# Three of seven inner products of an MLP's second product, taken for both token halves at once by a second seven-product scheme

## The chip, the cores and the metric

The kernel runs on one core of one Trainium2 chip. The metric is the device time of one execution in microseconds. A core has TensorE (PE: matmuls, with weight loads shown as PEld), VectorE (DVE), ScalarE (ACT), GpSimd (POOL) and SyncE (SP), which here issues nearly all DMAs. Each engine works off its own queue of instructions in order; they wait for each other at semaphores.

## The reference

One layer of an encoder over 2048 tokens of width 1024: a mixer (two kinds of attention, output projection, residual), then an MLP. Only the MLP matters here:

```python
h = rmsnorm(x, g_norm2[l]) * (1.0 + sc2) + sh2
x = x + gt2 * (jnp.square(jax.nn.relu(h @ w1[l])) @ w2[l])
```

w1 is 1024 x 4096, w2 is 4096 x 1024, all in float32.

## The kernel before

Everything is held transposed: features on the 128 partitions, tokens along the free axis, in four token blocks of 512 (`TB`). The MLP takes the tokens in two halves, `mb` 1 and then 0, each of two blocks. Within a half, each of the two MLP products is split into 2 x 2 blocks (output rows by tokens by contraction), and a Strassen-Winograd scheme makes the four block results from seven block products instead of eight. They are numbered 1 to 7 and taken in the order `PRODUCTS = (1, 6, 5, 7, 2, 3, 4)` (line 1283). The operands of products 3, 5, 6, 7 are sums and differences of blocks.

Precision: a float32 operand is split into two float32r parts, hi and lo (`split`, line 139: a cast on ScalarE, then a subtraction on VectorE), and `mm3` (line 206) issues three matmuls: hi by hi, hi by lo, lo by hi. Each is a 128 x 128 stationary tile against 512 moving columns.

The MLP is a list `steps` of objects, run in order by the loop at the end (line 1738 on). Before a step is run, its successors are prepared, that is, their operands split, as long as no more than eight operand tiles (pool `opp`, line 1289) are in use; each class says how many it takes and frees (`tiles`, `frees`). Jobs hung to a step number with `at(n, job)` (line 1325) are issued just before that step's matmuls; `later` holds jobs for some steps after. TensorE and SP keep the order of the program. The two classes of the MLP:

- `First` (line 1425), product with w1. A step is one product of one of 16 pairs of hidden tiles: 4 contraction tiles x 3 matmuls. The moving operands of all seven products stay in SBUF (`hops`, made by `right_blocks`, line 1363). The stationary sums are made on GpSimd (`sums`, line 1457). Relu, square and the sums that the second product needs of the hidden tiles are made on ScalarE and VectorE, and stored to DRAM as `scr_hid[mb, product, pair]` (`keep`).
- `Second` (line 1545), product with w2. A step is one of 16 contraction tiles of one product: 4 row blocks x 3 matmuls into four PSUM banks. Operands come from DRAM, two steps at a time: hidden tiles from `scr_hid`, weights from w2 or from the weight sums `scr_s` (`load`, line 1554), into one of four 8 KB buffers (`raw_pair`, line 1305). After a product's last step, `out` (line 1605) takes the banks: products 1, 6, 5, 7 build the running sums that Winograd's scheme needs (`s`, `u`, `v`, in the 12 buffers of `kept`), and 7, 2, 3, 4 finish an output block: `scalar_tensor_tensor` multiplies by the gate and adds to x, which `load_base` and `base` have brought in and to which they have added the running sum.

The weight sums `scr_s` are made once, during `First` of half 1, by `second_sums` (line 1525): per pair, four sums on VectorE and their stores. `norm2` (line 1331) computes the RMS norm of one token block: 8 loads, squares on ScalarE, adds on VectorE, four small matmuls (tile `pvm`), an inverse root on GpSimd, a diagonal on VectorE, four matmuls that spread it (tile `psr`). For half 0 it is hung at `end - 8` and `end`, `end` being the border between `First` and `Second` of half 1 (lines 1685, 1686), and `right_blocks` for half 0 follows at `end + 16 + 10 k`. The norm's and x's tiles come from `temp`, seven buffers.

In the profile's names: `oph`, `opv` are the split hidden and weight operands of `Second`, `opw` those of `First`, `w2s` the tile of `second_sums`, `tx` the x tiles, `ty` and `h` the right blocks, `ts` and `w` the sums of w1 on GpSimd. All instructions carry line 42, a helper's, so that groups are told apart by tile names.

Of the kernel before, what the change touches and what calls it, by code (L numbers as in the profile page):

```python
# [79 lines left out]
def encoder_kernel(ctx, tc, xT, c, g1, g2, w_in, w_rest, gqk, bias, w_o, w1, w2, w_ada, b_ada, out):  # L80
# [1200 lines left out]
    NP = DFF // P // 2  # L1281
    HK = KT // 2
    PRODUCTS = (1, 6, 5, 7, 2, 3, 4)
    scr_hid = scratch("scr_hid", [P, 2, TB], 2, 8, NP // 2)
    scr_s = scratch("scr_s", [P, 2, TB], 7, NP // 2)

    pm = ctx.enter_context(ExitStack())
    if True:
# [36 lines left out]
        def at(n, job):  # L1325
            jobs.setdefault(n, []).append(job)
# [4 lines left out]
        def norm2(tb, step):  # L1331
# [213 lines left out]
        class Second(Step):  # L1545
# [27 lines left out]
            def run(self):  # L1573
                mb, i, j = self.mb, self.i, self.j
                if j == 0:
                    Second.banks[i] = [bank(f"{self.nm}_{n}") for n in range(HK)]
                if i not in (1, 6, 5):
                    if j == NP // 2 - 1:
                        self.load_base()
                    if NP // 2 + 2 < j <= NP // 2 + 2 + HK:  # L1580
                        self.base(j - NP // 2 - 3)
# [10 lines left out]
            def load_base(self):  # L1592
                i, d = self.i, Second.whole
                for n in range(HK):
                    d["x", n] = temp(f"x{self.nm}_{n}")
                    sp.dma_start(d["x", n], scr_x[2 * self.mb + (i in (2, 4)), n + HK * (i in (7, 4))])

            def base(self, n):

                i, d = self.i, Second.whole  # L1600
                nn = n + HK * (i in (7, 4))
                x, u = d["x", n], d[{7: "v", 2: "s", 3: "v", 4: "u"}[i], n]
                dve.scalar_tensor_tensor(x, u, mod[:, 5 * KT + nn : 5 * KT + nn + 1], x, op0=ALU.mult, op1=ALU.add)

            def out(self, n, ps):
                i, d = self.i, Second.whole
                tb = 2 * self.mb + (i in (2, 4))
# [4 lines left out]
                if i == 6:  # L1612
                    d["u", n] = column_sum(dve, kept(f"u{self.nm}_{n}"), ps, d["s", n], ALU.add)
                    return
                if i == 5:
                    d["v", n] = column_sum(dve, kept(f"v{self.nm}_{n}"), ps, d["u", n], ALU.add)
                    return
                if i == 7:
                    column_sum(dve, d["u", n], ps, d["u", n], ALU.add)
                nn = n + HK * (i in (7, 4))  # L1620
                x = d["x", n]
                dve.scalar_tensor_tensor(x, ps, mod[:, 5 * KT + nn : 5 * KT + nn + 1], x, op0=ALU.mult, op1=ALU.add)
                sp.dma_start(out[nn * P : (nn + 1) * P, tb * TB : (tb + 1) * TB], x)

        class Mixed(Step):

# [44 lines left out]
        for mb in (1, 0):  # L1671
            begin = len(steps)
            steps += [First(mb, j, i) for j in range(NP) for i in PRODUCTS]
            for j in range(NP):
# [6 lines left out]
            if not mb:  # L1681
                at(begin - 8, steps[begin].load)
            if mb:
                end = len(steps)
# [6 lines left out]
            steps += [Second(mb, i, j) for i in PRODUCTS for j in range(NP)]  # L1691
            for n in range(begin + 7 * NP, len(steps), 2):
                at(n - 7 - max(0, begin + 7 * NP + 4 - n) // 2 * mb, steps[n].load)


        blocks = [right_blocks(1, k, kept if k else temp) for k in range(HK)]

# [100 lines left out]
```

## Time and profile before

| | us |
|---|---|
| median of 3 runs | 2598.27 |
| the three runs | 2595.89, 2599.91, 2598.27 |
| span of the profiled execution, first to last instruction | 2595.2 |
| First of half 1, from its first matmul (1365.9) | 305.8 |
| Second of half 1, from 1671.7 | 309.6 |
| First of half 0, from 1981.3 | 304.6 |
| Second of half 0, from 2286.0 | 304.8 |

The profiled execution's own time is not recorded apart from its span, which is 0.7 to 4.7 us shorter than the runs. In the rows below, a timeline row is: start in us, duration in us, engine, helper line, operation, output<-inputs, shapes, count, and in brackets the idle time before it and what ended it. A windows row is: stretch, its length, busy time (and number of instructions) of PE, PEld, DVE, ACT and POOL, granted clock of TensorE (1.00 is full), DMA share, GB/s. A row of grouped instructions ends in busy us, mean ns of one, and idle time before them. A wait row is: who <- for whom: us in total, times, longest.

### The profile page before, as it was taken

What the parts mean: (1) busy time and instruction counts of PE and PEld (TensorE: products, weight loads), DVE (VectorE), ACT (ScalarE), POOL (GpSimd) and SP (SyncE); (2) the same over time, 40 slices, a digit from 0 to 9 for tenths busy, and PEclk for the clock granted to TensorE, in tenths of its full rate; (3) what the DMA queues carried; (4) which work ended last, traced back from release to release, by engine and by line L of the source; (5) the groups of instructions that cost most, each with busy time, mean ns of one, the idle gap of its engine ahead of it and who ended that gap; (6) DMA issues with size and microseconds to landing.
All of it is one profiled execution on the core that took longest, in us unless ns stands there. A gap on an engine that the chain in (4) does not pass through costs nothing.

```text
span 2595.2 us, 39377 instructions
## 1 busy us (share of the span) xinstructions
PE 2571.3 (99%) x12628; PEld 2141.1 (83%) x12628; DVE 1886.0 (73%) x3233; ACT 1408.0 (54%) x2719; POOL 940.2 (36%) x1256
## 2 busy tenths in 40 slices
PE   9999999999999999999999999999999999999999
PEld 7888888888888888887888888888888888888887
DVE  7656767887799879998768777868766565655655
ACT  6333434668866686666744544556544544444443
POOL 4330154777766677776604333000002323200000
PEclk9999999999999999999999999999999999999999
DMA  9879879789887788756696777876764444375574
GB/s 350 333 295 364 329 293 280 222 246 273 267 257 242 237 276 249 256 172 208 207 363 244 264 266 249 308 263 240 253 228 172 142 153 156 128 267 196 193 272 154
DMA packets 251503, 640.20 MB, mean 247 GB/s; under 512 B 28576, under 2 KB 52128, under 8 KB 242208
## 3 DMA queue, kind: packets, MB, share of 16 engines
q1 hardware_dynamic: 250000, 632.96, 71.1%
q10 hardware_dynamic: 1296, 4.72, 0.4%
q8 instruction: 100, 1.64, 0.3%
q14 instruction: 107, 0.88, 0.1%
HBM read 446.20 MB, written 191.37 MB: 246 GB/s over the span
## 4 chain that ended last, share of the span: by engine, by line
PE 87%; DVE 5%; ACT 3%; issue 2%; DMA 2%; POOL 1%; SPq 1%; DVEq 0%; ACTq 0%; POOLq 0%
PE ps L42 45%; PE pt L42 11%; PE acc L42 6%; PE wt L42 6%; PE po L42 4%; PE z L42 4%; PE pf L42 4%; PE pq L42 3%; PE cz L42 2%; PE pso L42 2%; DVE p L42 2%; PE ct L42 1%; ACT z L42 1%; DVE wtl L42 1%; PE px L42 1%
## 5 line engine op out<-in xcount | busy, mean ns | idle before, releaser
L42 PE MATMUL ps<-oph,opv 128*128 128x512 f32 x2688 | 611.8, 389 | 0.2
L42 PE MATMUL ps<-h,opw 128*128 128x512 f32 x2664 | 605.2, 389 | 0.1
L42 PEld LDWEIGHTS ps<-oph,opv 128*128 128x128 f32 x2688 | 504.0, 188 | 106.1 <-DVE opv L42 0.8
L42 PEld LDWEIGHTS ps<-h,opw 128*128 128x128 f32 x2664 | 499.8, 188 | 105.2 <-DVE cx L42 0.9
L42 POOL TENSOR_TENSOR b<-p 128x512 f32<-128x512 f32 (+1 forms) x320 | 292.5, 914 | 167.9 <-DVE p L42 93.0
L42 ACT CAST wth<-wt 128x512 fp32r<-128x512 f32 (+3 forms) x544 | 257.4, 484 | 172.4 <-PE wt L42 162.4
L42 DVE TENSOR_TENSOR wtl<-wt,wth 128x512 fp32r<-128x512 f32 (+3 forms) x544 | 291.1, 547 | 59.3 <-ACT wth L42 56.8
L42 DVE TENSOR_TENSOR oph<-hw,oph 128x512 fp32r<-128x512 f32 x224 | 156.7, 700 | 214.4 <-ACT oph L42 214.3
L42 ACT CAST oph<-hw 128x512 fp32r<-128x512 f32 x224 | 139.3, 622 | 276.1 <-PE ps L42 266.0
L42 PE MATMUL pt<-w,ht 128*128 128x512 f32 x1248 | 288.2, 391 | 0.0
L42 POOL TENSOR_TENSOR ts<-w 128x512 f32<-128x512 f32 x32 | 44.0, 1375 | 666.3 <-DMA w<-in_w_dram 338.4
L42 PEld LDWEIGHTS pt<-w,ht 128*128 128x128 f32 x1248 | 233.0, 188 | 47.7
L42 DVE TENSOR_TENSOR_SCAN p<-z,p,zero 128x512 f32<-128x512 f32 x192 | 245.7, 1281 | 25.7 <-ACT z L42 18.8
L42 PE MATMUL acc<-wth,v 128*128 128x512 f32 (+3 forms) x544 | 220.6, 410 | 0.0
L42 ACT ACTIVATE z<-z 128x512 f32<-128x512 f32 (+1 forms) x320 | 166.5, 521 | 55.1 <-PE z L42 49.2
L42 PE MATMUL z<-k,q 128*128 128x512 f32 (+3 forms) x640 | 185.6, 371 | 7.6 <-DVE p L42 7.0
L42 PE MATMUL acc<-wtl,v 128*128 128x512 f32 (+3 forms) x544 | 185.4, 347 | 0.0
L42 DVE TENSOR_TENSOR opw<-w,opw 128x512 fp32r<-128x512 f32 x127 | 102.2, 807 | 113.2 <-ACT opw L42 113.1
L42 POOL TENSOR_TENSOR e<-e,cols 128x640 f32<-128x640 f32 (+4 forms) x128 | 143.0, 1123 | 83.2 <-DVE cols L42 57.0
L42 PE MATMUL wt<-ident,b 128*128 128x128 f32 x1088 | 171.4, 273 | 1.0 <-DVE cols L42 0.3
L42 PEld LDWEIGHTS wt<-ident,b 128*128 128x128 f32 x1088 | 136.4, 141 | 42.1 <-DVE cols L42 1.8
L42 PE MATMUL po<-fx,ow 128*128 128x512 f32 x576 | 161.6, 393 | 1.0 <-DMA ow<-scr_wo 1.0
(196 smaller groups left out, 4109.0 us busy)
## 6 DMA issues: line engine op xcount, KB each, us to landing
hw<-scr_hid SPq DMA_DIRECT2D x112, 512.0 KB, 3.8
q<-scr_q SPq DMA_DIRECT2D x128, 256.0 KB, 5.2
w<-in_w_dram SPq DMA_DIRECT2D x64, 512.0 KB, 5.3
hw<-scr_s SPq DMA_DIRECT2D x64, 512.0 KB, 4.6
k<-scr_k SPq DMA_DIRECT2D x240, 128.0 KB, 4.4
v<-scr_v SPq DMA_DIRECT2D x120, 256.0 KB, 4.0
wa<-in_w_ada_dram SPq DMA_DIRECT2D x48, 512.0 KB, 6.2
ow<-scr_wo SPq DMA_DIRECT2D x24, 1024.0 KB, 6.4
```

What stands on the lines that cost most here:

```text
L42: return lambda *x, **y: self.tc.keep_in_program_order(f(*x, **y))
```

## The change

`Second` keeps products 1, 6, 5, 7 for each half (`plain`). Products 2, 3 and 4 are no longer taken per half. Each of them, for both halves together, has a stationary matrix of 2048 x 512 (contraction by output rows) and 1024 moving tokens, and is split 2 x 2 again: contraction in two halves of 8 tiles, output rows in two halves of 256, tokens by `mb`. The seven products of that inner scheme are steps of a new class `Outer`: per product 8 steps, each 2 row blocks x 3 matmuls of 128 x 128 against 512 columns.

- The stationary sums of the inner scheme are made by `outer_sums` during the first 12 pairs of `First` of half 0 (four VectorE sums each) and kept in DRAM as `scr_t`.
- The moving operands are tiles `halves` of 128 x 2 x 512, which take the place of `hops` in SBUF. For each outer product, products 1, 5, 3, 2 of the inner scheme are loaded from `scr_hid` (`half`), and 5, 6, 7, 4 made by VectorE differences of 1024 elements (`half_sum`), at steps that a dictionary `plan` gives.
- The inner scheme's results stay in PSUM: product 2 adds to product 1's banks, 3 to 5's, and 6, 7, 4 to a copy of 1's that ScalarE makes. After each of 5, 6, 3, 7, 2, 4 the banks are weighed into the x tiles (`weigh`), which are stored when complete.
- The plain products' running sums are added to x as they come up, by `update`: x is loaded, weighed and, except for one output block, stored back to `scr_x`.
- Order: plain 1, 6, 5, 7 of half 1; `First` of half 0; plain 1, 6; outer 2; plain 5; outer 3; plain 7; outer 4.
- `norm2` of half 0 is spread three steps a tile and moved into `First` of half 1, to `begin + 18` and `begin + 48`; `right_blocks` of half 0 begins at `end + 1`.

The diff, cut to its core:

```diff
+    PLAIN = (1, 6, 5, 7)
+    OUTER = (1, 5, 6, 3, 7, 2, 4)
+    HOME = {1: 1, 2: 1, 5: 5, 3: 5, 6: 6, 7: 6, 4: 6}
+    HP = NP // 2
+    CN = TB // 2
...
-                at(step + k, lambda k=k: load(k))
-                at(step + k + 4, lambda k=k: add(k))
-            at(step + KT + 4, lambda: later.add(2, second))
+                at(step + 3 * k, lambda k=k: load(k))
+                at(step + 3 * k + 4, lambda k=k: add(k))
+            at(step + 3 * KT + 4, lambda: later.add(2, second))
...
             def out(self, n, ps):
...
+                if i == 6:
+                    column_sum(dve, d["s", n], ps, d["s", n], ALU.add)
+                if i == 5:
+                    d["v", n] = column_sum(dve, kept(f"v{self.nm}_{n}"), ps, d["s", n], ALU.add)
+                if i == 7:
+                    column_sum(dve, d["s", n], ps, d["s", n], ALU.add)
+                    x = d["x", 1, 1, n]
+                    weigh(x, ps, HK + n)
+                    sp.dma_start(rows_of(out, mb, HK + n, 0), x)
...
+        def plain(mb, i):
...
+            if i == 6:
+                update(mb, 0, 1, "s", spread(0, 1, 2, 6), spread(4, 5, 6, 10))
+            if i == 5:
+                update(mb, 0, 0, "v", spread(11, 12, 13, 14), spread(16, 17, 18, 19))
+            if i == 7:
+                update(mb, 1, 0, "v", spread(4, 5, 6, 7), spread(9, 10, 11, 12), False)
+                update(mb, 1, 1, "s", spread(10, 11, 12, 13), spread(16, 17, 18, 19))
...
+        class Outer(Step):
...
+                self.tiles, self.frees = 2 - k % 2, 1 + k % 2
...
+            def load(self):
+                i, pr = self.i, self.pr
+                t = Outer.raws[i, pr] = raw_pair([P, HP, CN], F32, f"l{self.nm}")
+                if (i, pr) in scr_t:
+                    sp.dma_start(t, scr_t[i, pr])
                     return
...
+            def prepare(self):
+                i, k = self.i, self.k
+                self.r = operand(halves[self.pr, k // 2][:, k % 2, :], f"r{self.nm}")
+                if k % 2 == 0:
+                    o = Outer.l = opp.tile([P, 2, 2, CN], F32R, tag="op", name=f"ol{self.nm}")
+                    split(o[:, 0], o[:, 1], Outer.raws[i, self.pr][:, k : k + 2, :])
+                self.l = Outer.l
...
+            def run(self):
+                pr, k = self.pr, self.k
+                home = HOME[pr]
+                for n in range(2):
...
+                    mm3(
+                        ps, self.l[:, 0, k % 2, ns], self.l[:, 1, k % 2, ns], self.r[:, 0, :], self.r[:, 1, :],
+                        k == 0 and not begun, k == HP - 1, begun,
+                    )
...
+        def half_sum(i, pr, g):
...
+            column_sum(dve, t, halves[x, g], halves[y, g], ALU.subtract)
...
+            for q in range(7):
+                at(f + HP * q - 12, steps[f + HP * q].load)
...
+                elif j < 12:
+                    outer_sums((2, 3, 4)[j // 4], j % 4, begin + 7 * j + 9)
...
-                norm2(1, end - 8)
-                norm2(0, end)
+                norm2(1, begin + 18)
+                norm2(0, begin + 48)
                 for k in range(HK):
-                    begins = end + 16 + 10 * k
+                    begins = end + 1 + 10 * k
...
+        f = plain(0, 1)
+        plain_loads(f, 7)
+        plain_loads(plain(0, 6), 7)
+        plan = {"load": {1: (f + 1, 3), 5: (f + 2, 3), 3: (f + 13, 2), 2: (f + 21, 2)}}
+        plan["sum"] = {5: (f + 6, 3), 6: (f + 17, 2), 7: (f + 20, 2), 4: (f + 25, 2)}
+        for i, p in ((2, 5), (3, 7), (4, None)):
+            f = outer(i, plan)
+            if p:
+                plain_loads(plain(0, p), 12)
+            e = f + 7 * HP
+            plan = {"load": {1: (f + 6, 2), 5: (f + 17, 2), 3: (f + 30, 2), 2: (f + 46, 2)}}
+            plan["sum"] = {5: (f + 23, 2), 6: (f + 36, 2), 7: (e + 2, 2), 4: (e + 5, 2)}
```

More of the change, by code (lines that the diff above doesn't have):

```diff
@@ L1590, in run @@
                         self.out(n, Second.banks[i][n])
[L1592 to L1603, printed above, removed]
             def out(self, n, ps):
-                i, d = self.i, Second.whole
-                tb = 2 * self.mb + (i in (2, 4))
+                mb, i, d = self.mb, self.i, Second.whole
                 if i == 1:
@@ new lines, in weigh, with rows_of, update, fetch @@
+        def weigh(x, a, n):
+            dve.scalar_tensor_tensor(x, a, mod[:, 5 * KT + n : 5 * KT + n + 1], x, op0=ALU.mult, op1=ALU.add)
+        def rows_of(t, mb, n, odd):
+            tb = 2 * mb + odd
+            return t[n * P : (n + 1) * P, tb * TB : (tb + 1) * TB]
+        def update(mb, r, odd, acc, loads, adds, keep=True):
+            d = Second.whole
+            def fetch(n):
+                d["x", r, 1 - odd, n] = x = (temp if keep else kept)(f"xu{mb}_{r}{odd}_{n}")
+                sp.dma_start(x, scr_x[2 * mb + odd, HK * r + n])
+            def add(n):
+                x = d["x", r, 1 - odd, n]
+                weigh(x, d[acc, n], HK * r + n)
+                if keep:
+                    later.add(1, lambda: sp.dma_start(scr_x[2 * mb + odd, HK * r + n], x))
+            for n in range(HK):
+                at(loads[n], lambda n=n: fetch(n))
+                at(adds[n], lambda n=n: add(n))
@@ new lines, in plain @@
+        def plain(mb, i):
+            f = len(steps)
+            steps.extend(Second(mb, i, j) for j in range(NP))
+            spread = lambda *ns: [f + n for n in ns]
+            if i == 6:
[5 more added lines that the diff above has]
+                update(mb, 1, 1, "s", spread(10, 11, 12, 13), spread(16, 17, 18, 19))
+            return f
```

113 lines of the change are left out of this document (91 added, 22 removed).

## The prediction

> **What bounds the kernel now.** I read the page first, for which engine is full, and then TensorE's timeline from the out-projection's last rows on, to see whether its matmuls stand one behind the other.
>
> ```profile
> PE 2571.3 (99%) x12628; PEld 2141.1 (83%) x12628; DVE 1886.0 (73%) x3233; ACT 1408.0 (54%) x2719; POOL 940.2 (36%) x1256
> PEclk9999999999999999999999999999999999999999
> ```
>
> ```profile
> 1365.89 5.62 PE L42 MATMUL ps<-h,opr 128*128 128x512 f32 x24
> 1371.35 300.50 PE L42 MATMUL ps<-h,opw 128*128 128x512 f32 x1320
> 1671.69 16.48 PE L42 MATMUL ps<-oph,opv 128*128 128x512 f32 x72
> 1688.01 0.95 PE L42 MATMUL pvm<-ones,r 128*128 128x1 f32 x8
> 1688.82 8.47 PE L42 MATMUL ps<-oph,opv 128*128 128x512 f32 x36
> ...
> 1981.32 304.80 PE L42 MATMUL ps<-h,opw 128*128 128x512 f32 x1344
> 2285.96 304.80 PE L42 MATMUL ps<-oph,opv 128*128 128x512 f32 x1344
> ```
>
> The MLP is four stages of 1344 matmuls: First and Second of half 1, then of half 0. First of half 0 runs from 1981.32 to 2285.96: 304.64 us, 0.22667 us a matmul, with no break in the row. Second of half 0 takes the same. First of half 1 takes 305.80 (1365.89 to 1671.69), so it stands still for 1.16 us; Second of half 1 takes 309.63, of which four groups of norm matmuls take some 0.81 each (1688.01 to 1688.82 is one), and 1.75 is standing still. Busy shares can't show this, since matmul ends are modelled; starts and counts can. So the MLP is bound by **the number of its matmuls**, to 3 us in 1225. A Second step (12 matmuls) takes 2.72 us. The other engines by stage, in the order PE, weight load, DVE, ACT, POOL:
>
> ```profile
> 1365.90:1671.70 305.80, 305.74 (x1346) 251.90 (x1345) 243.53 (x321) 146.38 (x260) 96.95 (x62) 1.00 0.75 263
> 1671.70:1981.30 309.60, 309.44 (x1377) 255.53 (x1376) 222.56 (x350) 163.76 (x289) 14.59 (x17) 1.00 0.68 245
> 1981.30:2286.00 304.70, 304.70 (x1346) 252.37 (x1345) 181.75 (x257) 146.73 (x252) 81.51 (x57) 1.00 0.44 155
> 2286.00:2590.80 304.80, 304.76 (x1345) 252.11 (x1343) 171.40 (x267) 128.62 (x226) 0.00 (x0) 1.00 0.60 212
> ```
>
> VectorE is 80% busy in the first and 56% in the last; that is the room that the change can spend.
>
> **What it removes.** Second before: 2 halves x 7 products x 16 contraction tiles x 4 row blocks x 3 = 2688 matmuls. After: products 1, 6, 5, 7 stay, 2 x 4 x 16 x 4 x 3 = 1536; products 2, 3, 4 become three outer products of 7 x 8 x 2 x 3 = 336 each, 1008. That is 2544, 144 fewer. They have the same shapes (128x128 against 128x512), so I take the same pace: 144 x 0.22667 = **32.6 us less**. An outer step has 6 matmuls, 1.36 us.
>
> The Trainium skill, "TensorE: Matmul & The Clock Gate", section "Back-to-back issue gap", puts a sustained stream of weight loads and matmuls at about 131 ns for 512 columns; by that the 144 would be worth 18.9 us. The stages above show 226.7 ns, and the measurement decides.
>
> **What it adds to VectorE, and whether TensorE waits for it.** Each operand that an outer step splits costs a cast on ScalarE and a subtraction on VectorE.
>
> ```profile
> 2400.40 0.62 ACT L42 CAST oph<-hw 128x512 fp32r<-128x512 f32 x1 [1.58 <-PE ps L42]
> 2400.93 0.61 ACT L42 CAST opv<-hw 128x512 fp32r<-128x512 f32 x1
> 2401.06 0.69 DVE L42 TENSOR_TENSOR oph<-hw,oph 128x512 fp32r<-128x512 f32 x1 [1.43 <-ACT oph L42]
> 2401.66 0.69 DVE L42 TENSOR_TENSOR opv<-hw,opv 128x512 fp32r<-128x512 f32 x1
> ...
> 2403.12 0.62 ACT L42 CAST oph<-hw 128x512 fp32r<-128x512 f32 x1 [1.58 <-PE ps L42]
> ```
>
> ```profile
> 2581.79 2.07 DVE L42 SCALAR_TENSOR_TENSOR tx<-cu,mod,tx 128x512 f32<-128x512 f32 x3
> ```
>
> ```profile
> L42 DVE TENSOR_TENSOR wol<-wo,woh 128x1024 fp32r<-128x1024 f32 x8 | 9.8, 1228 | 1.7 <-ACT woh L42 1.6
> ```
>
> Instructions overlap their neighbours: a subtraction lasts 0.69 but the next starts 0.60 after it; three weighings take 2.07, so 0.66 each; casts start 0.53 apart. A sum of two half tiles (1024 elements) lasts 1.23 in its nearest row; with the same overlap of 0.09 I take 1.14.
>
> One outer product has 56 steps, 76.2 us. VectorE's work in it: 84 operands (one moving tile a step, one stationary tile for two) x 0.605 = 50.8; 12 weighings x 0.66 = 7.9; four column sums of the plain product just ended, 2.4; half sums for the next outer product, 8 x 1.14 = 9.1 (in the first two); four late updates, 2.6 (in the last two); four weighings of product 7, 2.6 (in the last). That is 70.3, 72.9 and 66.4 of 76.2: it fits, at 92, 96 and 87%. ScalarE's 84 casts x 0.53 = 45 fit easily. What matters is crowding. The eight operand tiles reach 4 outer steps ahead, 5.44 us; a pair's casts and subtractions take about 2 of that, so VectorE may fall some 3.5 us behind.
> - Steps 23 to 30 (10.9 us): 12 operands, 4 half sums, 2 weighings = 13.1, so 2.3 late; steps 31 to 35 win back 0.9; 36 to 43 add 2.3 again: 3.6 late. At the edge; I take 0.5 for each of the first two outer products.
> - Start of the third: column sums and weighings of product 7, 4 x 1.27 = 5.1, wait for its banks and come ahead of step 4's operands (1.2), which are done about 6.1 after the border, when step 4 is due at 5.4; the updates in steps 0 to 3 add 0.4 a pair twice. I take 1.5.
>
> The DMAs stand beside this: an outer product moves 8.4 MB of half tiles, 7.3 MB of left tiles, 2.1 MB of x and 2.1 MB of output, 261 GB/s; the first plain product of half 0 with its half tiles 193 + 129 = 322 for twelve steps. The page's slices reach 364:
>
> ```profile
> GB/s 350 333 295 364 329 293 280 222 246 273 267 257 242 237 276 249 256 172 208 207 363 244 264 266 249 308 263 240 253 228 172 142 153 156 128 267 196 193 272 154
> ```
>
> I count them at nothing while they come in time (the third rival has the price if not). For VectorE together **2.5 us added**; between 0 and, by the second rival, 11.5.
>
> **What it moves.** The norm of half 0's tokens goes from the border into First of half 1. Its rsqrt runs on GpSimd, VectorE's diagonal is queued for it, and TensorE has the spreading matmuls three steps (8.2 us) behind the column sums.
>
> ```profile
> 1692.68 1.02 POOL L42 TENSOR_TENSOR nym<-nvm,mhalf 128x4 f32<-128x4 f32 x1 [55.27 <-DVE nvm L42]
> 1694.86 0.69 DVE L42 TENSOR_TENSOR ndgm<-ident,nym 128x512 f32<-128x512 f32 x1 [2.26 <-POOL nym L42]
> 1697.13 1.06 PE L42 MATMUL psr<-ndgm,ones 128*128 128x128 f32 x8
> ```
>
> ```profile
> 1495.70 1.30 POOL L42 TENSOR_TENSOR ts<-w 128x512 f32<-128x512 f32 x1 [10.62 <-DMA w<-in_w_dram]
> ...
> 1500.36 1.73 POOL L42 TENSOR_TENSOR ts<-w,ts 128x512 f32<-128x512 f32 x1
> ```
>
> At its old place GpSimd was free. The first norm's column matmuls now follow step 47, which ends at 1365.89 + 48 x 2.72 = 1496.5, inside GpSimd's run of four weight sums, 1495.70 to 1502.1. The rsqrt queues behind it, and the diagonal holds VectorE. The run's end plus 2.2 of rsqrt plus 0.7 is about 1505.0; the spread is due at 1504.7. The second norm, 30 steps later, meets a run that is nearly over. Bounds 0 and 6.4 (the run's length); I take **1.5**, with the 14 adds on a VectorE that is 80% busy. The norm matmuls themselves only move. Its 16 loads of 256 KB go through SP three steps apart, in a stage whose DMA share is 0.75, and take temporaries: seven, of which the weight sums use three in 7 steps; operands there are split 7 steps ahead, so a late one is no late matmul.
>
> The 48 weight sums for the outer products go into First of half 0, whose VectorE then stands at 181.75 plus 29 (48 x 0.605) or, if each meets GpSimd, plus 82 (48 x 1.70, from the row below). Both fit in 304.7.
>
> ```profile
> 1636.18 1.78 DVE L42 TENSOR_TENSOR w2s<-w2s 128x512 f32<-128x512 f32 x1
> ```
>
> First of half 1 has 64 such sums and stands still for 1.16 us; 48/64 of it is **0.9**; bounds 0 and 1.75, the most that any stage loses now.
>
> Half 1's plain products carry half 0's right blocks in 64 steps where there were 112, but the blocks keep their spacing of 10 steps, and the loads that stood in their way go.
>
> ```profile
> 1825.38 8.63 SPq L42 DMA_DIRECT2D tx<-scr_x  x4
> ...
> 1831.28 4.86 PEld L42 LDWEIGHTS ps<-oph,opv 128*128 128x128 f32 x22 [0.41 <-DVE opv L42]
> ...
> 1837.48 4.63 PEld L42 LDWEIGHTS ps<-oph,opv 128*128 128x128 f32 x21 [0.42 <-DVE opv L42]
> ```
>
> The new updates (4 weighings) fall among blocks 1 and 2. Old stall 1.75; bounds 0 and twice that; I take 2.05, **0.3 more**. The end has two weighings and stores behind the last matmul for four: **0.3 less** (bounds 0 and 0.6).
>
> Sum: -32.6 + 2.5 + 1.5 + 0.9 + 0.3 - 0.3 = **-27.7 us**. The profiled execution has a span of 2595.2, so 2567.5 after; the runs' median, 2598.27, lies 3.1 above that span, and the same difference gives **2570.5**.
>
> **The rivals.**
> - *Nothing new stands still.* The crowding stays inside the operands' lead. Only the 32.6 and the 0.3 count: 2565.4. For it: no sum above exceeds its stage. Against it: both present stalls come from such crowding, at 80% or less. 12%.
> - *VectorE's instructions don't overlap in the outer products* as they do in pairs, so each costs its duration: 0.69, 0.745, 1.23. Steps 23 to 30 then need 14.7 for 10.9, and by step 43 VectorE is 7.5 late, 4.0 beyond the lead, in two outer products; the third's start is about 3.1 late; with 0.4 at the second's, 11.5 instead of 2.5: 2579.5. Against it: chains of several instructions already start 0.60 apart. For it: more reads of half tiles and waits between them. 19%. The Trainium skill, "VectorE: DVE Perf Modes", section on the TRN2 errata, says that SBUF latency is exposed between instructions and paid once for each; by that rule this rival would hold. The 0.60 above speaks against it.
> - *Slower: SP's queue holds back the outer products' left tiles.* SP issues everything in order. A left tile (1 MB, partly in runs of 1 KB) is placed 12 steps, 16.3 us, ahead and split 4 steps ahead, which leaves 10.9.
>
> ```profile
> wr<-in_w_in_dram SPq DMA_DIRECT2D x5, 1024.0 KB, 8.9
> ow<-scr_wo SPq DMA_DIRECT2D x24, 1024.0 KB, 6.4
> ```
>
> ```profile
> SPq L42 <- DVE opv L42: 307.3, 83, 8.8
> SPq L42 <- DVE ca L42: 135.6, 31, 6.3
> ```
>
> Landing in 8.9 leaves 2.0. A store that waits for a weighing, or an x load that waits for a temporary, in front of it costs what exceeds 2.0, 21 times: it eats the gain from a hold of 3.6 us on, and is slower by over 0.2% from 3.8. With the 4.4 of the second row (135.6/31) the time is 2598.3 - 32.6 + 21 x 2.4 = 2616. Holds of the mean 3.7 of the first row come out within 0.2%. Against it: SP waits there because it runs ahead of TensorE, and operands waited for a load only five times in the MLP:
>
> ```profile
> ACT oph L42 <- DMA hw<-scr_hid: 10.1, 5, 5.7
> ```
>
> 8% slower, 5% even.
>
> **How the numbers follow.** Forecast 56%, no new stall 12%, no overlap 19%: 87% faster by over 0.2% (5.2 us, about what a measurement of this kernel can tell from no change). 5% within it, 8% slower. The range takes the lower bounds together (the no-stall case less the present stalls, some 2562) and, above, the no-overlap rival with the norm's bound half spent (2579.5 + 2.5, and 2 for the spread of the runs): 2562 to 2584.
>
> **What would show it.** 12484 matmuls; each outer product 336 in 76.2 us, with gaps only near steps 25 to 45 and at the third's start, ended by VectorE; one short gap at the first norm's spread; First of half 0 a little over 304.64; DVE near 90% in the outer products, with subtractions starting 0.60 apart. It is wrong if TensorE's waits name a DMA or a bank, if an outer matmul isn't 0.2267, or if the outer products' gaps are above 5 us each.

## The result, and the profile after

The changed kernel takes 2583.63 us (median of 4 runs, 2583.49 to 2586.42), the kernel before beside it 2597.08 (4 runs): a ratio of 0.995, 95% interval 0.9936 to 0.9964. That is faster, by 0.5%. The profiled spans are 2581.9 and 2595.2, so 13.3 us less where 27.7 were forecast. Run once more (`after_again`, below), the kernel came to 2585.21, ratio 0.996 (0.9946 to 0.9975).

The page of the changed kernel has the predicted 12484 matmuls, and VectorE's share rises from 73 to 79%:

```profile
PE 2546.8 (99%) x12484; PEld 2112.9 (82%) x12484; DVE 2031.6 (79%) x3401; ACT 1448.3 (56%) x2785; POOL 950.4 (37%) x1256
```

TensorE's timeline of the changed kernel shows where the gain went. A row is an unbroken run of matmuls; a new row means other operands, or a wait in brackets.

```profile
1365.86 5.60 PE L42 MATMUL ps<-h,opr 128*128 128x512 f32 x24
...
1478.56 13.89 PE L42 MATMUL ps<-h,opw 128*128 128x512 f32 x60 [0.48 <-DVE cx L42]
1492.92 5.75 PE L42 MATMUL ps<-h,opw 128*128 128x512 f32 x24 [0.47 <-ACT cu L42]
1498.51 0.95 PE L42 MATMUL pvm<-ones,r 128*128 128x1 f32 x8
1499.32 8.46 PE L42 MATMUL ps<-h,opw 128*128 128x512 f32 x36
1510.56 1.13 PE L42 MATMUL psr<-ndgm,ones 128*128 128x128 f32 x8 [2.78 <-DVE ndgm L42]
...
1589.03 8.47 PE L42 MATMUL ps<-h,opw 128*128 128x512 f32 x36
1599.66 1.16 PE L42 MATMUL psr<-ndgm,ones 128*128 128x128 f32 x8 [2.17 <-DVE ndgm L42]
...
1685.93 66.33 PE L42 MATMUL ps<-oph,opv 128*128 128x512 f32 x289
...
1771.08 16.51 PE L42 MATMUL ps<-oph,opv 128*128 128x512 f32 x61 [1.59 <-ACT opv L42]
...
1867.20 201.74 PE L42 MATMUL ps<-h,opw 128*128 128x512 f32 x888
...
2174.11 87.20 PE L42 MATMUL ps<-oph,opv 128*128 128x512 f32 x384
2261.15 21.92 PE L42 MATMUL ps<-opr,ol 128*128 128x512 f32 x96
...
2337.37 43.68 PE L42 MATMUL ps<-oph,opv 128*128 128x512 f32 x192
2380.89 21.92 PE L42 MATMUL ps<-opr,ol 128*128 128x512 f32 x96
...
2457.07 43.68 PE L42 MATMUL ps<-oph,opv 128*128 128x512 f32 x192
2500.59 22.70 PE L42 MATMUL ps<-opr,ol 128*128 128x512 f32 x96
2523.13 11.04 PE L42 MATMUL ps_s<-opr,ol 128*128 128x512 f32 x48
```

The starts give each stage's length, and the count of matmuls times 0.22667 what it needs; the rest is standing still. First of half 1: 1685.93 - 1365.86 = 320.07, less 304.64 and less 3.24 for the norm's matmuls, which now stand there: **12.19 still, where 1.16 were**. Plain products of half 1: 1867.20 - 1685.93 = 181.27 for 768 matmuls (174.08): **7.19 still, where 1.75 were**. First of half 0: 306.91, so 2.27 still, where nothing was. Outer products: 76.22, 76.18, and about 0.8 lost in the third's first 16 steps (22.54 to the next row for 21.76). Against the kernel before, then, the stages stand still for 11.0 + 5.4 + 2.3 + 0.8 us more, and the end takes 0.2 less: of the 32.6 us saved, 13.3 are left.

The windows of First of half 1 and of the three outer products (PE, weight load, VectorE, ScalarE, GpSimd):

```profile
1365.90:1685.90 320.00, 311.78 (x1377) 254.66 (x1376) 255.37 (x341) 153.59 (x273) 103.42 (x73) 1.00 0.74 262
...
2261.20:2337.40 76.20, 76.20 (x338) 63.02 (x337) 70.01 (x106) 50.56 (x86) 0.00 (x0) 1.00 0.67 237
2380.90:2457.10 76.20, 76.20 (x338) 63.06 (x337) 71.39 (x109) 50.12 (x86) 0.00 (x0) 1.00 0.70 249
2500.60:2577.60 77.00, 77.00 (x337) 62.56 (x335) 63.92 (x101) 47.10 (x80) 0.00 (x0) 1.00 0.40 144
```

Here is the puzzle. In the first two outer products VectorE is 92 and 94% busy and TensorE doesn't wait. In First of half 1 it is 80% busy (255.37 of 320.00), and TensorE stands still for 12 us.

**Theory A.** The busy share hides that VectorE was full there before. VectorE's timeline of the kernel before, one pair of First of half 1 (other sums, each started as the one before ends, are left out):

```profile
1560.74 0.68 DVE L42 TENSOR_TENSOR cv<-ps,cv 128x512 f32<-128x512 f32 x1
1563.29 0.69 DVE L42 TENSOR_TENSOR opw<-w,opw 128x512 fp32r<-128x512 f32 x1 [1.87 <-ACT opw L42]
...
1574.43 0.69 DVE L42 TENSOR_TENSOR opw<-w,opw 128x512 fp32r<-128x512 f32 x1 [1.87 <-ACT opw L42]
...
1580.14 0.68 DVE L42 TENSOR_TENSOR cv<-ps,cv 128x512 f32<-128x512 f32 x1
```

From one `cv` to the same one a pair later VectorE takes 1580.14 - 1560.74 = 19.40, all of it back to back but for two waits of 1.87 for casts on ScalarE. TensorE needs 84 x 0.22667 = 19.04 for the pair. So VectorE falls behind a little in such a pair, and how far shows in what it releases. ScalarE's copy of product 1's bank comes behind a VectorE sum, and product 2, three steps (8.16 us) after product 1's end, needs that bank. One such copy and the weight load that waited for it, in the kernel before, late in First of half 1:

```profile
1643.47 0.58 ACT L42 COPY cu<-ps 128x512 f32<-128x512 f32 x1
1644.10 1.92 PEld L42 LDWEIGHTS ps<-h,opw 128*128 128x128 f32 x9 [0.48 <-ACT cu L42]
```

and in First of half 0, right after its first step, which ends at 1984.04:

```profile
1984.24 0.59 ACT L42 COPY cu<-ps 128x512 f32<-128x512 f32 x1 [1.58 <-PE ps L42]
```

Pair 14's product 1 ends at about 1635.2, so the copy comes 8.3 us late, at the end of its lead; in half 0 it comes 0.2 late. Pair 14's is the latest: by the same reckoning the other copies of First of half 1 come 4.6 to 7.7 us late, 6.8 already in the first pair, and those of First of half 0 from 0.2 to 1.2. Most of the lead is in use from the start, and it is gone in the late pairs. Theory A: the lead in First of half 1 was all but used up, so what is added to VectorE's chain there is paid in TensorE's time. Its rivals were **B**, that only the norm's spreading matmuls wait, for an inverse root that comes late, and **C**, for the plain products, that SP's queue is held by the new stores to `scr_x`. **D** and **E** came up later, and are told where they were tried.

### The profile page after: what moved, and what is told of

The parts are those of the page before. It is cut to its first block, busy times and chain, and to the rows that moved or that the text cites. A ratio compares the mean times of both kernels' runs of the same rounds, so it can differ in the third digit from the quotient of the medians.

```text
span 2581.9 us, 39420 instructions
## 1 busy us (share of the span) xinstructions
PE 2546.8 (99%) x12484; PEld 2112.9 (82%) x12484; DVE 2031.6 (79%) x3401; ACT 1448.3 (56%) x2785; POOL 950.4 (37%) x1256
## 5 line engine op out<-in xcount | busy, mean ns | idle before, releaser
L42 PE MATMUL ps<-oph,opv 128*128 128x512 f32 x1536 | 353.3, 391 | 2.7 <-ACT opv L42 1.6
L42 PEld LDWEIGHTS ps<-oph,opv 128*128 128x128 f32 x1536 | 289.0, 188 | 66.3 <-ACT opv L42 2.7
L42 DVE TENSOR_TENSOR_SCAN p<-z,p,zero 128x512 f32<-128x512 f32 x192 | 245.9, 1282 | 25.7 <-ACT z L42 18.3
L42 DVE TENSOR_TENSOR oph<-hw,oph 128x512 fp32r<-128x512 f32 x128 | 90.4, 706 | 80.0 <-ACT oph L42 80.0
L42 ACT CAST opr<-r 128x512 fp32r<-128x512 f32 x168 | 104.7, 625 | 83.2 <-PE ps L42 46.6
```

The lines of the kernel that those rows point to most:

```text
L42: return lambda *x, **y: self.tc.keep_in_program_order(f(*x, **y))
```

## The experiments

### The norm's move: back, later, and alone

`norm_back`: the changed kernel with the norm and the right blocks where they were, and in half 1 the last x tile of each of the updates in products 6 and 5 loaded and weighed four to five steps later (this part of the edit is left out here).

```diff
-                at(step + 3 * k, lambda k=k: load(k))
-                at(step + 3 * k + 4, lambda k=k: add(k))
+                at(step + k, lambda k=k: load(k))
+                at(step + k + 4, lambda k=k: add(k))
...
-                norm2(1, begin + 18)
-                norm2(0, begin + 48)
+                norm2(1, end - 8)
+                norm2(0, end)
...
-                    begins = end + 1 + 10 * k
+                    begins = end + 16 + 10 * k
```

> The norm of half 0 and its right blocks stand where they stood before the change (norm at the border, one step a tile; right blocks from 16 steps after it); two updates of half 1 get later steps so that their temporaries fit. All else is the changed kernel. Theory A (VectorE and ScalarE together are full in First of half 1, so that whatever is put there is paid): First of half 1 falls from 320.1 to 305 to 307 us, the plain products of half 1 take 177 to 183 with the norm's matmuls in them, and the time falls by 9 to 13 us to 2571 to 2575. Rival: if First of half 1 loses its time to something else that the change brings (other code, loads that run ahead), it stays above 315 and the time within 3 us of the changed kernel.

2568.87 us, ratio 0.9896 (0.9881 to 0.9911). That is below the 2571 to 2575 that theory A gave. Its interval lies below that of the changed kernel's 0.995; of the kernels here with the whole output it is the fastest, level with `norm_back_late` (below). TensorE's timeline of `norm_back`:

```profile
1365.88 0.61 PE L42 MATMUL ps<-h,opr 128*128 128x512 f32 x2
...
1673.08 16.48 PE L42 MATMUL ps<-oph,opv 128*128 128x512 f32 x72
...
1855.51 14.67 PE L42 MATMUL ps<-h,opw 128*128 128x512 f32 x64
```

First of half 1 is 307.20, so 12.9 shorter than in the changed kernel. The plain products take 182.43 with the norm's 3.24, so 5.1 still instead of 7.2.

`spread_late`: the changed kernel with the spreading matmuls seven steps behind the column sums instead of three.

```diff
-                later.add(3, third)
+                later.add(7, third)
```

> The changed kernel with the norm's spreading matmuls issued seven steps behind the column sums instead of three. Rival B (the loss in First of half 1 is TensorE waiting in front of the two spreads, 3.1 + 2.5 us, and what that makes late): First of half 1 falls by 5 us or more, to 309 to 315. Theory A: TensorE no longer waits there, but the work that made it wait is still queued, so the waits turn up at product 2 of the next pairs (behind ScalarE's copy of product 1): First of half 1 falls by 0 to 3 us, to 317 to 320.

2584.69, ratio 0.9956 (0.9941 to 0.9971): no gain. TensorE's timeline of `spread_late`:

```profile
1366.95 5.60 PE L42 MATMUL ps<-h,opr 128*128 128x512 f32 x24
...
1494.84 5.74 PE L42 MATMUL ps<-h,opw 128*128 128x512 f32 x24 [1.56 <-ACT cu L42]
...
1521.55 1.06 PE L42 MATMUL psr<-ndgm,ones 128*128 128x128 f32 x8
...
1606.91 5.78 PE L42 MATMUL ps<-h,opw 128*128 128x512 f32 x24 [2.12 <-DVE cx L42]
...
1689.35 65.80 PE L42 MATMUL ps<-oph,opv 128*128 128x512 f32 x289
```

The spread no longer waits, and First of half 1 takes 322.40 all the same, above even the 317 to 320 of theory A: the lost time turned up at product 2's bank (1.56) and at VectorE's sums (2.12). B falls. When an engine is behind, taking one wait away only shows the next.

`norm_moved_alone`: the kernel before, with nothing of the change but the norm's move.

```diff
-                at(step + k, lambda k=k: load(k))
-                at(step + k + 4, lambda k=k: add(k))
-            at(step + KT + 4, lambda: later.add(2, second))
+                at(step + 3 * k, lambda k=k: load(k))
+                at(step + 3 * k + 4, lambda k=k: add(k))
+            at(step + 3 * KT + 4, lambda: later.add(2, second))
...
-                norm2(1, end - 8)
-                norm2(0, end)
+                norm2(1, begin + 18)
+                norm2(0, begin + 48)
```

> The kernel before with one part of the change alone: the norm of half 0 moved into First of half 1 with three steps a tile; the right blocks stay at 16 steps after the border and no outer products are there. Theory A: First of half 1 goes from 305.8 to 320 as in the changed kernel; Second of half 1 loses its 3.2 us of norm matmuls and up to 1 us of waits; the time is 8 to 11 us above the kernel before, 2605 to 2608. If the move is harmless by itself and only hurts beside the new loads, First of half 1 stays below 312 and the time within 4 us of before.

2610.51, ratio 1.0054 (1.0037 to 1.0071): the move alone is slower, by 14.4 us against the 2596.11 of the kernel before beside it. By its starts First of half 1 grows from 305.80 to 325.92, and Second of half 1 shrinks by 3.8, of which 3.24 are the norm's matmuls. That is the direction of A, and more than it forecast (320, and 2605 to 2608). The stage is 3 to 6 us longer than with the whole change (320.07, and 322.54 in `after_again`); where that comes from is seen at the end of the next part.

### How much lead is there: sums that nobody needs

Eleven `tensor_tensor` adds of 128 x 512 on VectorE, one a pair, into a tile that nobody reads; on the kernel before, in First of half 1 (`extra_add_half1`) and in First of half 0 (`extra_add_half0`, with `mb == 0` in the last condition).

```diff
+        def extra():
...
+            dve.tensor_tensor(idle[0], idle[0], idle[0], op=ALU.add)
...
+                if mb == 1 and 3 <= j < 14:
+                    at(begin + 7 * j + 4, lambda: extra())
```

> The kernel before with 11 additional VectorE sums of 128 x 512 on a tile of their own, one in each of the pairs 3 to 13 of First of half 1 (no DMA, nothing waits for them; they compute nothing that is used). Theory A (First of half 1 is full although VectorE shows 80% there): after the first one or two have eaten the remaining lead, each costs TensorE 0.6 to 1.7 us; First of half 1 goes from 305.8 to 311 to 320 us and the time up by 5 to 14 us. Rival (the 20% idle time of VectorE can be used, and the moved norm cost through its loads, temporaries and waits): up by 0 to 2 us.

2608.57, ratio 1.0041 (1.0026 to 1.0056). TensorE's timeline of `extra_add_half1`:

```profile
1365.11 0.61 PE L42 MATMUL ps<-h,opr 128*128 128x512 f32 x2
...
1533.60 38.63 PE L42 MATMUL ps<-h,opw 128*128 128x512 f32 x168 [1.55 <-ACT cu L42]
...
1682.98 16.48 PE L42 MATMUL ps<-oph,opv 128*128 128x512 f32 x72
```

317.87 for 305.80: **12.1 us for eleven sums, 1.10 each**, in a stage whose VectorE was 80% busy. The wait names product 1's copy again.

> The kernel before with the same 11 sums in First of half 0, where VectorE is 60% busy. Both theories: no change, First of half 0 stays at 304.6 us and the time within 2 us of before. A loss here would say that the price of such a sum has nothing to do with how full the stage is.

2596.35, ratio 0.9999 (0.9989 to 1.0009), and First of half 0 stays at 304.64: the same sums at the same steps cost nothing where VectorE is 60% busy (181.75 of 304.7). This pair of runs is what A rests on.

Theory **E** was that the price lies in the collision of VectorE's sums with GpSimd's, so that it is paid whichever of the two engines makes the sum. `extra_add_gpsimd` has the same eleven adds on GpSimd, in First of half 1.

```diff
-            dve.tensor_tensor(idle[0], idle[0], idle[0], op=ALU.add)
+            pool.tensor_tensor(idle[0], idle[0], idle[0], op=ALU.add)
```

> As extra_add_half1, but the 11 additional sums stand on GpSimd, which is 32% busy in that stage and nobody waits for the sums. Theory E (VectorE's loop in First of half 1 is long because its instructions take 1.7 us instead of 0.6 while GpSimd adds, so that GpSimd's work there is paid too): each sum of 1.3 to 1.7 us slows one VectorE instruction by 1.1 us; First of half 1 goes from 305.8 to 311 to 318 us. Rival (only VectorE's own instructions count): 305 to 307 us, the time within 2 us of before.

2600.03, ratio 1.0013 (1.0003 to 1.0023); the stage takes 307.77, 2.0 more. That is hardly more than its spread: in `extra_add_half0`, whose code for this stage is that of the kernel before, it takes 307.47. The profiled execution is the quickest of its ten (2597.45), so the stage may lose more in the others. Even so, the eleven sums cost far less on GpSimd than on VectorE. What a collision costs the run can't say, because the added sums hardly made VectorE longer: it is busy for 243.97 in the stage, and for 243.53 in the kernel before. E, as a price of the collision, stays untested by it. The collision itself is real, as VectorE's and GpSimd's timelines of this kernel show:

```profile
1500.85 1.74 POOL L42 TENSOR_TENSOR ts<-w,ts 128x512 f32<-128x512 f32 x1
1501.36 1.78 DVE L42 TENSOR_TENSOR w2s<-w2s 128x512 f32<-128x512 f32 x1
1502.55 1.49 POOL L42 TENSOR_TENSOR idle<-idle 128x512 f32<-128x512 f32 x1
1503.07 0.68 DVE L42 TENSOR_TENSOR cv<-ps,cv 128x512 f32<-128x512 f32 x1
```

A sum of two SBUF tiles takes 1.78 while GpSimd adds; the next, with one operand in PSUM (`ps`), takes 0.68 beside a GpSimd add. The Trainium skill, "SBUF — State Buffer", section "Who interferes with whom", says that `tensor_tensor` with both inputs in SBUF contends with GpSimd's reads for a shared port; these rows agree.

**Busy time and idle time add up.** The windows of First of half 1 in `norm_moved_alone`, `extra_add_half1` and `extra_add_gpsimd` (VectorE is the third engine), and the row of waits that costs VectorE most in this stage of the kernel before:

```profile
1366.25:1692.17 325.92, 316.22 (x1378) 256.73 (x1376) 261.80 (x341) 153.50 (x273) 102.73 (x73) 0.99 0.74 258
1365.10:1683.00 317.90, 308.87 (x1346) 251.01 (x1345) 256.77 (x334) 146.75 (x260) 98.70 (x63) 1.00 0.71 253
1364.51:1672.28 307.77, 307.42 (x1345) 251.23 (x1344) 243.97 (x321) 146.74 (x260) 109.36 (x75) 1.00 0.74 260
```

```profile
DVE opw L42 <- ACT opw L42: 58.4, 36, 1.9
```

The stage less VectorE's busy time is 64.1, 61.1 and 63.8 here, 62.3 in the kernel before (305.80 - 243.53) and 64.6 in the changed kernel (320.00 - 255.37). This idle time doesn't shrink when work is added, for most of it is the waits for casts: 58.4 us before, 55.6 in the changed kernel. So the stage grows by about what VectorE's busy time grows by: 11.9 busy and 11.0 still in the changed kernel, 18.3 and 16.9 in `norm_moved_alone`, 13.2 and 12.1 in `extra_add_half1` (all over the kernel before, and without the norm's matmuls of 3.24). This also tells why the norm's move alone costs more. VectorE has 341 instructions there as in the changed kernel, but by its timelines 48 of its sums last over 1 us, as they do beside a GpSimd add, where 43 do in the changed kernel. So time that collisions add to VectorE seems to be paid like any other; no run here changes it alone.

### The plain products of half 1

`x_store_late`: the changed kernel, where half 1's update in product 6 stores to `scr_x` four steps after the weighing instead of one, and its fourth x tile is loaded and weighed four steps later.

```diff
-                    later.add(1, lambda: sp.dma_start(scr_x[2 * mb + odd, HK * r + n], x))
+                    later.add(4 if mb and acc == "s" and not r else 1, lambda: sp.dma_start(scr_x[2 * mb + odd, HK * r + n], x))
...
-                update(mb, 0, 1, "s", spread(0, 1, 2, 6), spread(4, 5, 6, 10))
+                update(mb, 0, 1, "s", spread(0, 1, 2, 10 if mb else 6), spread(4, 5, 6, 14 if mb else 10))
```

> The changed kernel, where the updates of half 1 during product 6 store their x tiles four steps after the weighing instead of one, and the fourth x tile is loaded four steps later. Theory C (SP stood still in front of such a store behind a late weighing, so that the operands' loads behind it came late): the plain products of half 1 fall from 181.3 to 176 to 179 us, the time by 2 to 5 us. Rival (ScalarE and VectorE waiting for each other in the right blocks set the loss, not the loads): 180 to 182, no change in the time.

2580.73, ratio 0.994 (0.9925 to 0.9955); the plain products take 178.10 instead of 181.27. Against the changed kernel the intervals of the whole time overlap, but the stage is 3.2 shorter, where 181.27, 181.15 and 180.42 (`spread_late`) are its times with the updates unchanged. C is supported; one tile's load and weighing were moved with the stores, so the stores' own part isn't set apart.

`after_no_updates` leaves half 1's updates in products 6 and 5 out altogether, so that this share of the output is missing. `after_again`, the changed kernel once more, ran beside it.

```diff
-                update(mb, 0, 1, "s", spread(0, 1, 2, 6), spread(4, 5, 6, 10))
+                mb or update(mb, 0, 1, "s", spread(0, 1, 2, 6), spread(4, 5, 6, 10))
```

(and the same for product 5's).

> The changed kernel without half 1's updates of x in plain products 6 and 5 (8 loads, weighings and stores; their share of the output is left out). Theory C (SP standing in front of the updates' stores and loads sets most of the 7.2 us that the plain products of half 1 stand still): the stage falls from 181.3 to 175 to 177.5 us. Rival (the right blocks, packed nearer to the border, set it by themselves): 179.5 to 182.

> The changed kernel once more, for how far the stages of one kernel differ between executions. Expected: First of half 1 320 to 324 us, plain products of half 1 181 to 182, First of half 0 305 to 307, the time 2583 to 2585.

2578.99, ratio 0.9935 (0.992 to 0.995), beside 2585.21, ratio 0.996 (0.9946 to 0.9975). TensorE's timeline of `after_no_updates`:

```profile
1687.06 96.94 PE L42 MATMUL ps<-oph,opv 128*128 128x512 f32 x421
...
1863.59 304.80 PE L42 MATMUL ps<-h,opw 128*128 128x512 f32 x1344
```

The plain products take 176.53, 2.45 still; `after_again` has 181.15. So the updates cost 4.6 to 4.7 of the 7.2; of the rise of 5.4 over the kernel before, that leaves 0.7. How they do it is seen in the changed kernel, in SP's and ScalarE's timelines:

```profile
1754.37 0.42 SPq L42 DMA_DIRECT2D hw<-scr_hid  x1
...
1761.02 0.62 ACT L42 CAST oph<-hw 128x512 fp32r<-128x512 f32 x1 [6.18 <-DMA hw<-scr_hid]
```

and in its waits:

```profile
SPq L42 <- DVE txu L42: 36.8, 6, 18.4
```

SP stands in front of the stores until VectorE has weighed their tile `txu`, 18.4 us at the longest. The loads of the next operands are queued behind, with a right block's four loads, go out at 1754.37, and ScalarE's cast waits 6.18 for one. TensorE's 1.59 at 1771.08 comes after that, with a right block's jobs on ScalarE (1765.49 to 1769.99) between the late cast and the operand that TensorE waits for. So the block has a part in it; without the updates the wait is gone.

### What is left in norm_back

Four kernels, all built on `norm_back`, went after the 5.1 us that its plain products still lose. Theory **D** was that the right blocks, ten steps apart there, crowd VectorE at the stage's end.

`blocks_apart`: blocks eleven steps apart, later stores and x loads (only the blocks' part of the edit is shown).

```diff
...
-                    begins = end + 16 + 10 * k
+                    begins = end + 16 + 11 * k
```

> The kernel norm_back with half 0's right blocks 11 steps apart instead of 10, the updates of half 1 in products 6 and 5 storing four steps after the weighing, and their last x tiles loaded later, so that less falls together. Theory C (crowding of right blocks, updates and stores at SP sets the rest of the loss in half 1's plain products): they fall from 182.4 to 178 to 181 us and the time by 1 to 4 us, to 2565 to 2568. If the right blocks alone set it, 181.5 to 183 and no change.

2577.22, ratio 0.9922 (0.9907 to 0.9937): worse. The last blocks now fall on the column sums of a product (VectorE has them from 1816.26, right behind a block's subtractions; TensorE waits 1.73 at 1819.39) and on GpSimd's sums for the next stage (from 1848.51 on; VectorE's instructions take 1.75 from 1851.82 to 1858.6). TensorE's timeline of `blocks_apart`:

```profile
1855.29 0.79 PE L42 MATMUL ps<-oph,opv 128*128 128x512 f32 x1 [3.45 <-DVE oph L42]
```

`blocks_clear`: each block's jobs put by hand clear of the column sums, the updates' weighings in between (the updates' part of the edit is left out here).

```diff
...
-                    begins = end + 16 + 10 * k
-                    for n, job in zip((0, 5, 7, 9), right_blocks(0, k, temp)):
-                        at(begins + n, job)
+                    for n, job in zip(((13, 18, 20, 22), (23, 26, 28, 30), (31, 36, 38, 40), (41, 50, 52, 54))[k], right_blocks(0, k, temp)):
+                        at(end + n, job)
```

> The kernel norm_back with the jobs of half 0's right blocks placed by hand so that none falls on the end of a plain product (steps 16, 32, 48 from the border, where the column sums are) or on GpSimd's weight sums near step 60, and the updates' weighings of half 1 placed between the blocks. Same work. Theory D (the plain products of half 1 lose time where a right block, whose casts make ScalarE and VectorE wait for each other, meets the column sums or the updates): the stage falls from 182.4 to 178 to 180 us, the time by 2 to 5 us, to 2564 to 2567. Rival (each block costs its wait wherever it stands): 181 to 183, the time within 1.5 us of norm_back.

2573.23, ratio 0.9915 (0.9902 to 0.9929); the stage takes 183.36 and the waits have moved to 1757 to 1771. D, in this form, falls.

`norm_back_late`: the updates' stores four steps after the weighing instead of one, and the last x tile of product 5's update loaded two steps later and weighed one step later (left out here).

```diff
...
-                    later.add(1, lambda: sp.dma_start(scr_x[2 * mb + odd, HK * r + n], x))
+                    later.add(4 if mb and not r else 1, lambda: sp.dma_start(scr_x[2 * mb + odd, HK * r + n], x))
```

> The kernel norm_back with the updates of half 1 storing four steps after the weighing instead of one, as in x_store_late, and the fourth x tile of product 5 loaded two steps later. If SP's hold in front of the stores still costs there: the plain products of half 1 fall from 182.4 to 179 to 181 and the time to 2565 to 2568. If not: no change, 2568 to 2571.

2569.8, ratio 0.9896 (0.988 to 0.9911): no gain; the stage takes 184.34.

`no_updates`: half 1's updates in products 6 and 5 left out, as above, with their share of the output.

> The kernel norm_back without half 1's updates of x in plain products 6 and 5 (8 loads, weighings and stores; their share of the output is left out). If the updates set the rest of the loss in half 1's plain products (5.1 us in norm_back against 1.75 in the kernel before, with the same right blocks): the stage falls from 182.4 to 178 to 180. If the right blocks' own waits set it: 181.5 to 183.

2567.62, ratio 0.9887 (0.9871 to 0.9903); the stage takes 181.89, 4.6 still. So with the norm at its old place the updates are not what is left; what is stays open.

### The outer products' lead

`outer_lead6`: `norm_back` with six operand tiles instead of eight in use ahead of an outer step.

```diff
-            while nxt is not None and ready - used + nxt.tiles <= 8:
+            while nxt is not None and ready - used + nxt.tiles <= (6 if isinstance(nxt, Outer) else 8):
```

> The kernel norm_back with at most six instead of eight operand tiles ahead in the outer products. By the prediction's sum VectorE falls 3.6 us behind in steps 23 to 43 of the first two outer products and 0.7 to 1.5 at the third's start; with three steps of lead, about 2.1 us to spare, that shows as 1 to 2 us in each and 2 to 3 at the third's start, 4 to 7 us in all. If VectorE keeps up better than summed there, the outer products stay at 76.2 us and the time within 1.5 us of norm_back.

2571.26, ratio 0.9905 (0.989 to 0.992), 2.4 us more than `norm_back`. The wait at the third outer product's start, in TensorE's timeline of `outer_lead6`:

```profile
2489.47 20.32 PE L42 MATMUL ps<-opr,ol 128*128 128x512 f32 x83 [0.82 <-DVE opr L42]
```

The first two outer products take 76.78 and 76.83, and the third's first 16 steps 24.1 for 21.76: 3.6 lost in all, where `norm_back` loses 0.8 and 4 to 7 were expected. The wait shown names VectorE, and it stands where the prediction's sum of crowding had one; so do the losses in steps 32 to 47 of the first two, where it had VectorE 3.6 us behind by step 43. With the lead of eight tiles the crowding is nearly all absorbed.

## Why the prediction was wrong

The direction was right, the size was not: 13.3 us less where 27.7 were forecast. That the time lies just within the stated range is luck: its upper end, 2584, was worked out from the rival without overlap, which did not come. By the prediction's own steps:

- **The 144 matmuls**: right; 32.64 us, and every outer product at 0.2267 a matmul.
- **Crowding in the outer products**: 2.5 forecast, 0.8 measured, all of it at the third's start, which had been put at 1.5. VectorE was busy for 70.0, 71.4 and 63.9 where 70.3, 72.9 and 66.4 were worked out. The 0.5 in each of the first two did not come. The rival in which instructions don't overlap is refuted: VectorE's load at those stages is that of 0.60 a subtraction, and it fits.
- **The norm's move**: the step that failed; 1.5 forecast with bounds 0 and 6.4, 11.0 measured. It went wrong in two places. First, it looked for the delay in GpSimd's run of weight sums alone, and not in VectorE's own queue. VectorE's timeline of the changed kernel:

```profile
1503.32 1.77 DVE L42 TENSOR_TENSOR opw<-ts,opw 128x512 fp32r<-128x512 f32 x1
...
1507.31 0.15 DVE L42 TENSOR_SCALAR nvm<-pvm 128x4 f32<-128x4 f32 x1
1509.72 0.69 DVE L42 TENSOR_TENSOR ndgm<-ident,nym 128x512 f32<-128x512 f32 x1 [2.26 <-POOL nym L42]
```

  The column matmuls begin at 1498.51, and VectorE takes their result only at 1507.31, behind what it already had in its queue. GpSimd's run of weight sums, which came later than before, had ended at 1506.25, so at this spread that queue would have held the root up too, but VectorE came last. GpSimd then answers in 2.26, as it did at the old place. At the second norm the run was over, as the step had said, and GpSimd stood idle for 7.04 us until VectorE took the column sums at 1596.51. The spread, due at 1499.32 + 36 x 0.22667 = 1507.48, starts at 1510.56; the second at 1599.66 for 1597.19. These two are 5.5 us. Second, the other 5.5 are mostly at product banks and sums (`cu`, `cx`). For these the step has no term: it put the 14 adds into the 1.5 because VectorE was 80% busy, and looked at late loads only ("a late one is no late matmul"). The lead that it counted on, operands split 7 steps ahead, was not the one that mattered; that of product 1's copy, 8.2 us, was nearly spent before anything was added (6.8 us late in the first pair, 8.3 in pair 14). What the runs showed in its place: the stage pays for what is added to VectorE's busy time, here 11.9 us. The bound of 6.4 covered one queue only, and so was no bound. The prediction named a wait for a bank as a sign that it is wrong, and that sign came.
- **The plain products of half 1**: 0.3 forecast, bounds up to 1.75, 5.4 measured. The likely mechanism was in the text, as the third rival's, SP held by a store behind a weighing, but it was priced for the outer products alone, where it did not happen; the updates in half 1 issue the same stores, and the step that put those updates at 0.3 looked at VectorE's blocks and not at SP's queue.
- **The weight sums in First of half 0**: 0.9 forecast, 2.3 measured, 0.5 above its bound of 1.75. First of half 0 takes 304.64 in some of the changed kernels (`spread_late`, `after_no_updates`, `blocks_apart`) and 305.3 to 307.6 in others with the same code there, so this term has no better price than 0 to 3.
- **The end**: 0.3 less forecast, 0.2 measured.

The two mis-sized steps are the miss: together 14.7 us over their forecast, where the whole is 14.4. `norm_back`, which takes the norm out of the first of them, lands at 2568.87, 1.6 below the forecast. That is in part luck: its plain products still lose 3.4 us more than before, where 0.3 was forecast, and its outer products 1.7 less.

Open are: what makes `norm_back`'s plain products still lose 5.1 us; how much of the updates' price is the stores' and how much the weighings'; and what decides between 304.64 and 307 in First of half 0. Moving the weight sums off GpSimd, so that VectorE's sums would not meet them, wasn't tried.

## What to carry to other kernels

A busy share is not slack. Before work is added to an engine, look up how late its releases already come against when they are needed (here copies 4.6 to 8.3 us late of an 8.2 us lead at an 80% share, 0.2 to 1.2 late at 60%), and ask what the idle time consists of: waits that come back with every pass can't be filled. Where the lead is gone, price each added instruction at its full time. A store that waits for an engine holds every load queued behind it, wherever it stands: price it in every stage that gets one, and not only in the one that the change is about.

## What the runs showed of the hardware

- A VectorE sum of two SBUF tiles of 128 x 512 takes 0.68 to 0.69 us alone and 1.77 to 1.79 when GpSimd adds all the while; with one operand in PSUM it takes 0.68 in either case.
- The same eleven sums cost 1.10 us each in one stage and nothing in another of the same loop. In the first, VectorE's busy time grew by 13.2 us and its idle time went only from 62.3 to 61.1.
